# Seven products for the last MLP group too, and two of four operand sums by adding transfers

## The chip, the cores and the metric

The kernel runs on one core of a Trainium2 chip. The metric is the device time of one execution in microseconds; the kernel before has a median of 2015.0 us over three runs (2014.59 to 2015.04). The engines are named as in the profile: PE (TensorE, matrix products; PEld its weight loads), DVE (VectorE), ACT (ScalarE), POOL (GpSimd), SP (SyncE, which issues transfers). A line of the program is written L802.

## The reference

Two layers of an encoder on 256 tokens of width 2048, all in float32. Each layer normalises, projects, runs three kinds of attention, projects back, and then adds a squared-ReLU MLP; a last normalisation follows. The change is in the second product of the MLP, with `w_down`:

```python
for l in range(DEPTH):
    ...
    x = x + jnp.einsum('bse,ed->bsd', mix, w_o[l])
    h = rmsnorm(x, norm_mlp[l])
    u = jax.nn.relu(jnp.einsum('bsd,df->bsf', h, w_up[l]))
    x = x + jnp.einsum('bsf,fd->bsd', u * u, w_down[l])
return rmsnorm(x, norm_final)
```

`w_up[l]` is 2048 x 8192 and `w_down[l]` 8192 x 2048.

## The kernel before

**Numbers.** PE multiplies in a reduced float32 format. To keep float32 accuracy each operand is held as a high part (rounded to that format) and a low part (what is left), and a product is three matmuls: high x high, low x high, high x low. A weight tile of 128 x 1024 is loaded raw (512 KB, tile `wraw`, five buffers), split by ACT, which makes the high part (`whi`, L988), and by DVE, which makes the low part (`wlo = raw - whi`, L989); `whi` and `wlo` have three buffers each.

**Steps.** All weight work is one list of steps, carried out in order by one loop over it. At step i the loads up to step i+6 have been issued, the splits up to i+2, and the preparations (`prep`) up to i+4; then the step's matmuls are issued, and small pieces of other work follow (transposes, attention). The order in which the instructions then stand on each engine is set by a scheduler that moves independent instructions past each other; each engine carries out its own in that order.

**The MLP.** The 8192 hidden columns are cut into eight groups of 1024. `up_steps(g)` makes group g in four pieces q of 256 columns (four steps each, 16 steps in all, L691 and L696); an evacuation on ACT and DVE gives `uT[q]`, the squared activations as high and low part. `down_steps` multiplies a group by `w_down` in the plain way, one 512-column block j of the output at a time (four steps of 12 matmuls, L477), and adds the result to `x` (L739). Groups run one behind the other: while group g goes through `w_down`, group g+1 goes through `w_up`.

**Seven products.** In groups 0 to 6 the output columns 0 to 1023 (j = 0 and 1) are done another way, in `strassen_steps`. The operand is taken as 2 x 2 blocks A11 to A22 (two blocks of tokens, two halves of the rows) and the weight as B11 to B22, and the product is formed from seven block products (P1 to P7, two steps of six matmuls each, L802) in place of eight. For that, sums of blocks are needed on both sides. Those of the activations (`sums_of`, tiles `sT`) are made by DVE and ACT in the evacuation of each piece q, but not for q of 28 and over, which belong to group 7. Those of the weights are four DVE sums of 128 x 1024 for each of two halves h: B12 onto B11 (L815), B22 + B11 (`t2`, L817), B22 onto B12 (L821), and B21 onto `t2` (L832). The blocks are loaded into tiles of their own: B11 into `spare`, the others into `side` (four buffers). Three PSUM banks collect the products (`a` and `d`, the two halves of the tile `S`, and `b`); after each product DVE adds a bank to `x` or subtracts it (L782). The eight plain steps of j = 2 and 3, and the 16 steps of `up_steps(g+1)`, lie between the steps of the seven products, by the list `order` (1 is a step of a product, 0 another one).

**Group 7** goes through `w_down` the plain way for all four column blocks, after everything else. When a column block of `x` is complete, `layer_end` starts what follows: in layer 0 the transposes for the next layer, in layer 1 the squares and the gain of the last normalisation. The very last column block of layer 1 is done one token block at a time, so that the output can begin early.

Of the kernel before, what the change touches and what calls it, by code (L numbers as in the profile page):

```python
# [23 lines left out]
P = 128  # L24
D = 2048
# [18 lines left out]
def tile_trunk(ctx: ExitStack, tc: tile.TileContext, x_in, w_in, w_o, w_up, w_down,  # L44
# [459 lines left out]
    def layer_steps(l):  # L504
# [152 lines left out]
        def up_steps(g):  # L657

            out_, evacs = [], []
            for q in range(4 * g, 4 * g + 4):  # L660
                box = {}

                def evac(q=q, box=box):
# [14 lines left out]
                    if q < 28:  # L678
                        sums_of(q, a)
# [40 lines left out]
        def down_steps(g, js):  # L720
            out_ = []
            for j in js:
                box = {}
                for k in range(4):
                    def mm(wh, wl, j=j, k=k, box=box):
                        if k == 0:
                            box["b"] = [mm_bank(), mm_bank()]
                            box["w"] = []
                        final = l == L - 1 and g == 7 and j == 3
                        hts = [uT[4 * g + k]] * 2  # L730
                        mode_b(box["b"], hts, wh, wl, [0, 1], k == 0, k == 3, blocks=(0,) if final else (0, 1),
                               lo_last=g < 7)
                        box["w"].append((hts, wh, wl))
                        if k < 3:
                            return

                        def evac(t):
                            xs = x[:, t, j * 512:(j + 1) * 512]
                            nc.vector.tensor_add(xs, xs, box["b"][t])  # L739
                        if final:  # L740
                            evac(0)
                            final_block(0)
                            tail = [mm_bank(), mm_bank()]
                            for c in range(2):
                                cols = slice(c * 256, c * 256 + 256)
                                for i, (hts, vh, vl) in enumerate(box["w"]):
                                    mode_b([None, tail[c]], hts, vh[:, :, cols], vl[:, :, cols], [0, 1],
                                           i == 0, i == 3, n=256, blocks=(1,))
                                xs = x[:, 1, 1536 + c * 256:1792 + c * 256]
                                nc.vector.tensor_add(xs, xs, tail[c][:, 0:256])  # L750
                                square_cols(1, 1536 + c * 256, 256, fin["ss"][:, 7 + c:8 + c])
                            final_block(1)
                            return
                        evac(0)
                        evac(1)
                        if g == 7:
                            layer_end(l, j)
                    out_.append(Step(w_down[l, (g * 4 + j) * 4 + k], 2, 512, None, mm, fourth=g == 7))
            return out_

        def strassen_steps(g):
# [5 lines left out]
            raw, t2, box = {}, {}, {}  # L767
# [11 lines left out]
            def evac(bank, t, j, sign):  # L779
# [5 lines left out]
            plan = [("P1", "A11", "a", True, (0, 0, 1)), ("P6", "S2", "a", False, (1, 0, 1)),  # L785
                    ("P7", "S3", "d", True, (1, 1, -1)), ("P5", "S1", "a", False, (1, 1, -1)),
                    ("P3", "S4", "a", False, (0, 1, -1)), ("P2", "A12", "b", True, (0, 0, 1)),
                    ("P4", "A22", "d", False, (1, 0, 1))]
            out_ = []
            for name, lf, bk, fresh, dst in plan:  # L790
                for h in range(2):
                    def mm(wh, wl, name=name, lf=lf, bk=bk, fresh=fresh, dst=dst, h=h):
# [12 lines left out]
                        if h == 1:  # L805
                            evac(o, *dst)
                    loads, prep, get = [], None, None
# [11 lines left out]
                    elif name == "P7":  # L819
                        def prep(h=h):  # L820
                            nc.vector.tensor_add(raw["B12", h], raw["B12", h], raw["B22", h])  # L821
# [353 lines left out]
```

## Time and profile before

| | |
|---|---|
| median of three runs | 2015.0 us (2014.59 to 2015.04) |
| profiled execution | 2015.19 us, of which the span of its instructions is 2013.4 us |
| PE busy | 2000.6 us, 10264 matmuls |
| DVE busy | 1618.2 us |
| ACT busy | 1200.9 us |
| POOL busy | 290.6 us, none of it in the MLP's groups |
| HBM read | 377.34 MB |

The span is what the profile counts from; a few microseconds around it belong to the time as well (2015.19 - 2013.4 = 1.8 us). The MLP of layer 0 runs from about 319 to 1006 us, that of layer 1 from 1317 to 2005 us, and a middle group takes 85.5 us. Matmuls are pipelined, so one's own duration (about 390 ns) is longer than the time from one start to the next, which is what counts.

### The profile page before, as it was taken

What the parts mean: (1) busy time and instruction counts of PE and PEld (TensorE: products, weight loads), DVE (VectorE), ACT (ScalarE), POOL (GpSimd) and SP (SyncE); (2) the same over time, 40 slices, a digit from 0 to 9 for tenths busy, and PEclk for the clock granted to TensorE, in tenths of its full rate; (3) what the DMA queues carried; (4) which work ended last, traced back from release to release, by engine and by line L of the source; (5) the groups of instructions that cost most, each with busy time, mean ns of one, the idle gap of its engine ahead of it and who ended that gap; (6) DMA issues with size and microseconds to landing.
All of it is one profiled execution on the core that took longest, in us unless ns stands there. A gap on an engine that the chain in (4) does not pass through costs nothing.

```text
span 2013.4 us, 27963 instructions
## 1 busy us (share of the span) xinstructions
PE 2000.6 (99%) x10264; PEld 1706.0 (85%) x10264; DVE 1618.2 (80%) x2112; ACT 1200.9 (60%) x1732; POOL 290.6 (14%) x336
## 2 busy tenths in 40 slices
PE   9999999999999999999999999999999999999998
PEld 7888888888888888888888888888888888888887
DVE  6677877879888898887657688778888888888875
ACT  6667756565555556555656677565655556555554
POOL 0684520000000000000008745100000000000001
PEclk9999999999999999999999999999999999999999
DMA  7745655565575656656666456555665756657554
GB/s 276 226 154 162 209 170 190 168 217 193 178 228 170 219 184 192 215 172 198 189 184 200 152 176 198 176 189 179 192 215 170 231 167 210 205 169 233 166 167 156
DMA packets 110102, 384.97 MB, mean 191 GB/s; under 512 B 12515, under 2 KB 16867, under 8 KB 109964
## 3 DMA queue, kind: packets, MB, share of 16 engines
q1 hardware_dynamic: 109532, 382.08, 59.8%
q8 instruction: 81, 1.33, 0.3%
q10 hardware_dynamic: 432, 1.10, 0.2%
q14 instruction: 57, 0.47, 0.1%
HBM read 377.34 MB, written 2.11 MB: 188 GB/s over the span
## 4 chain that ended last, share of the span: by engine, by line
PE 98%; ACT 1%; DVE 0%; issue 0%; DMA 0%; SPq 0%; DVEq 0%; POOLq 0%; POOL 0%
PE mm L477 44%; PE mm L691 23%; PE mm L696 12%; PE S L802 11%; PE mm L802 2%; PE tr L392 1%; PE tr L411 1%; PE S L355 1%; PE S L354 1%; PE tr L221 1%; PE tr L404 0%; ACT big L372 0%; PE tr L267 0%; DMA x<-in_x_dram 0%; PE tr L283 0%
## 5 line engine op out<-in xcount | busy, mean ns | idle before, releaser
L989 DVE TENSOR_TENSOR wlo<-wraw,whi 128x1024 fp32r<-128x1024 f32 (+1 forms) x531 | 654.6, 1236 | 212.5 <-ACT whi L988 209.9
L988 ACT CAST whi<-wraw 128x1024 fp32r<-128x1024 f32 (+1 forms) x531 | 556.7, 1051 | 418.1 <-PE mm L691 170.2
L477 PE MATMUL mm<-whi,big 128*128 128x512 f32 (+1 forms) x2252 | 643.8, 386 | 0.5 <-ACT whi L988 0.5
L691 PE MATMUL mm<-big,whi 128*128 128x512 f32 x2048 | 509.5, 391 | 0.0
L477 PEld LDWEIGHTS mm<-whi,big 128*128 128x128 f32 x2252 | 418.6, 188 | 83.5 <-ACT whi L988 2.5
L691 PEld LDWEIGHTS mm<-big,whi 128*128 128x128 f32 x2048 | 377.1, 188 | 74.1
L477 PE MATMUL mm<-wlo,big 128*128 128x512 f32 (+1 forms) x1126 | 374.9, 384 | 0.0
L696 PEld LDWEIGHTS mm<-big,wlo 128*128 128x128 f32 x2048 | 279.4, 190 | 20.0
L696 PE MATMUL mm<-big,wlo 128*128 128x256 f32 x2048 | 285.5, 282 | 0.0
L477 PEld LDWEIGHTS mm<-wlo,big 128*128 128x128 f32 x1126 | 211.8, 188 | 39.6
L802 PE MATMUL S<-whi,big 128*128 128x512 f32 x672 | 182.2, 393 | 0.0
L477 PE MATMUL mm<-spare,big 128*128 128x512 f32 (+1 forms) x678 | 157.8, 381 | 0.0
L988 ACT CAST whi<-side 128x1024 fp32r<-128x1024 f32 x84 | 88.2, 1050 | 95.2 <-PE mm L691 77.8
L477 PEld LDWEIGHTS mm<-spare,big 128*128 128x128 f32 x678 | 122.3, 188 | 23.2
L802 PEld LDWEIGHTS S<-whi,big 128*128 128x128 f32 x672 | 119.1, 189 | 18.7
L989 DVE TENSOR_TENSOR wlo<-side,whi 128x1024 fp32r<-128x1024 f32 x84 | 102.7, 1223 | 37.5 <-ACT whi L988 37.1
L257 POOL TENSOR_TENSOR sm<-sm,mhalf 128x2 f32<-128x2 f32 (+2 forms) x14 | 15.3, 1092 | 793.7 <-DVE sm L252 773.9
L988 ACT CAST whi<-big 128x1024 fp32r<-128x1024 f32 x56 | 59.0, 1053 | 85.1 <-DVE big L817 36.4
L870 POOL TENSOR_TENSOR x<-x,big 128x512 f32<-128x512 f32 x6 | 8.6, 1451 | 669.5 <-ACT mid L877 669.5
L802 PE MATMUL S<-wlo,big 128*128 128x512 f32 x336 | 103.9, 390 | 0.0
L383 POOL TENSOR_SCALAR big<-big,sm 128x256 f32<-128x256 f32 x128 | 90.3, 723 | 3.0
L989 DVE TENSOR_TENSOR spare<-wraw,spare 128x1024 fp32r<-128x1024 f32 x54 | 70.2, 1299 | 22.2 <-ACT spare L988 21.7
(151 smaller groups left out, 2081.3 us busy)
## 6 DMA issues: line engine op xcount, KB each, us to landing
wraw<-in_w_up_dram SPq DMA_DIRECT2D x256, 512.0 KB, 4.1
wraw<-in_w_down_dram SPq DMA_DIRECT2D x144, 512.0 KB, 3.7
wraw<-in_w_in_dram SPq DMA_DIRECT2D x119, 512.0 KB, 3.8
side<-in_w_down_dram SPq DMA_DIRECT2D x84, 512.0 KB, 4.2
wraw<-in_w_o_dram SPq DMA_DIRECT2D x64, 512.0 KB, 3.6
spare<-in_w_down_dram SPq DMA_DIRECT2D x28, 512.0 KB, 4.2
side<-in_rpb_dram SPq DMA_DIRECT2D x32, 174.8 KB, 5.1
side<-avec SPq DMA_DIRECT2D x8, 384.0 KB, 5.4
```

The lines of the kernel that those rows point to most:

```text
L221: tr = nc.tensor.transpose(psv[:, kk, t, :], x[:, t, c0:c0 + P], ident).ins
L354: nc.tensor.matmul(o, st, u.kh[:, kh, :], start=True, stop=False)
L355: nc.tensor.matmul(o, st, u.kl[:, kh, :], start=False, stop=True)
L383: nc.gpsimd.tensor_scalar(p[:, s, :], p[:, s, :], rs[:, s:s + 1], 1.0, op0=ALU.mult, op1=ALU.mult)
L392: nc.tensor.transpose(ps[:, c * P:(c + 1) * P], u.p[:, s, kb * P:(kb + 1) * P], ident)
L411: nc.tensor.matmul(ps, u.V[:, kb, u.kv, :, :], pt[:, kb, :], start=n == 0, stop=n == 3)
L477: return nc.tensor.matmul(banks[t][:, 0:n], a, (wl if part == "hl" else wh)[:, i, :], start=first and i == 0 and part == "hh", stop=last a ...
L691: nc.tensor.matmul(box["b"][fs], wh[:, kk, fs * P:(fs + 1) * P], ht, start=s == 0 and kk == 0, stop=False, skip_group_check=True)
L696: nc.tensor.matmul(box["b"][fs][:, 0:256], wl[:, kk, fs * P:(fs + 1) * P], ht[:, 0:256], start=False, stop=s == 3 and kk == 3, skip_group_ ...
L802: nc.tensor.matmul(o, ops[i][a], w[:, i, :], skip_group_check=True, start=fresh and h == 0 and i == 0 and a == 0 and w is wh, stop=h == 1 ...
L988: act = nc.scalar.copy(h[:, part], w[:, part]).ins
L989: last_lo[0] = nc.vector.tensor_sub(lo[:, part], w[:, part], f(h[:, part])).ins
```

## The change

Group 7's columns 0 to 1023 are done by seven products as well. For that its rows' sums are made for all q, and its weights are packed like the other groups'. Group 6's plain half (j = 2 and 3) is taken out of group 6, where only the 16 steps of `up_steps(7)` now lie between the products, and is put between the products of group 7: j = 2 of groups 6 and 7 as one accumulation of eight steps, then j = 3 of group 6; j = 3 of group 7 stays last. The column blocks are thereby complete in another order: 2, 1, 0, 3.

In all groups two of the four sums of weights are no longer made by DVE. B12 is added onto B11 in its tile, and B21 onto `t2`, by transfers that add to what they find (`on_top`), issued by POOL. B12 and B21 are also needed by themselves, so each is now transferred twice. The products' order becomes P1, P2, P7, P6, P5, P3, P4.

```diff
-                    if q < 28:
-                        sums_of(q, a)
+                    sums_of(q, a)
...
-        def down_steps(g, js):
-            out_ = []
-            for j in js:
-                box = {}
-                for k in range(4):
-                    def mm(wh, wl, j=j, k=k, box=box):
...
+        def down_steps(gs, j):
+
+            out_, box = [], {}
+            tiles = [(g, k) for g in gs for k in range(4)]
+            final = l == L - 1 and gs == (7,)
+            for n, (g, k) in enumerate(tiles):
+                def mm(wh, wl, g=g, k=k, n=n):
...
-            plan = [("P1", "A11", "a", True, (0, 0, 1)), ("P6", "S2", "a", False, (1, 0, 1)),
-                    ("P7", "S3", "d", True, (1, 1, -1)), ("P5", "S1", "a", False, (1, 1, -1)),
-                    ("P3", "S4", "a", False, (0, 1, -1)), ("P2", "A12", "b", True, (0, 0, 1)),
+            plan = [("P1", "A11", "a", True, (0, 0, 1)), ("P2", "A12", "b", True, (0, 0, 1)),
+                    ("P7", "S3", "d", True, (1, 1, -1)), ("P6", "S2", "a", False, (1, 0, 1)),
+                    ("P5", "S1", "a", False, (1, 1, -1)), ("P3", "S4", "a", False, (0, 1, -1)),
                     ("P4", "A22", "d", False, (1, 0, 1))]
+
+            def on_top(tile, par, j, h):
+
+                nc.gpsimd.dma_start(tile, src(par, j, h).rearrange("p (k n) -> p k n", k=2), accum_op=ALU.add)
...
                         if h == 1:
                             evac(o, *dst)
+
+                            if g == 7 and name in ("P3", "P4"):
+                                layer_end(l, dst[1])
...
+                    elif name == "P2":
+                        def prep(h=h):
+                            assert ("P1", h) in done
+                            on_top(raw["B11", h], 0, 1, h)
+                    elif name == "P7":
+                        loads = [(("B12", h), src(0, 1, h), None), (("B22", h), src(1, 1, h), None)]
+
+                        def prep(h=h):
+                            nc.vector.tensor_add(raw["B12", h], raw["B12", h], raw["B22", h])
+                        get = lambda h=h: raw["B12", h]
                     elif name == "P6":
-                        loads = [(("B12", h), src(0, 1, h), None), (("B22", h), src(1, 1, h), None)]
-
                         def prep(h=h):
-                            nc.vector.tensor_add(raw["B11", h], raw["B11", h], raw["B12", h])
                             t2[h] = big(F32, 2, 512)
                             nc.vector.tensor_add(t2[h], raw["B22", h], raw["B11", h])
                         get = lambda h=h: t2[h]
...
+                    elif name == "P5":
+                        def prep(h=h):
+                            assert ("P6", h) in done
+                            on_top(t2[h], 1, 0, h)
                         get = lambda h=h: raw["B11", h]
...
                     else:
-                        def prep(h=h):
-                            nc.vector.tensor_add(t2[h], raw["B21", h], t2[h])
                         get = lambda h=h: t2[h]
...
-                    stp = Step(None, 2, 512, None, mm, fourth=False, prep=prep, raw=get,
+                    stp = Step(src(1, 0, h) if name == "P2" else None, 2, 512, None, mm, fourth=False, prep=prep,
+                               raw=operand if get else None,
                                loads=[(raw, k, v, w) for k, v, w in loads])
...
         steps.extend(up_steps(0))
-        for g in range(7):
-            ss = down_steps(g, (2, 3)) + up_steps(g + 1)
+        for g in range(8):
+
+            if g < 6:
+                ss = down_steps((g,), 2) + down_steps((g,), 3) + up_steps(g + 1)
+            elif g == 6:
+                ss = up_steps(7)
+            else:
+                ss = down_steps((6, 7), 2) + down_steps((6,), 3) + down_steps((7,), 3)
             hs = strassen_steps(g)
 
             order = [0, 0]
             for p_ in range(7):
-                order += [1, 0, 1] + ([0, 0] + [0] * (p_ in (1, 3, 5)) if p_ < 6 else [])
+                order += [1, 0, 1]
+                if p_ < 6:
+                    order += [0] * (2 if g < 6 else g == 6) + [0] * (g != 6 and p_ in (1, 3, 5))
+            order += [0] * (len(ss) - order.count(0))
...
-        steps.extend(down_steps(7, range(4)))
```

How the instructions move is shown at three places. A row is its line, its operation and its tiles, with the number of each buffer, and what it waits for in brackets (`DMASW` is a transfer that POOL issued, `DMAHW` one that SP issued). The lines of the changed kernel are numbered on: the split on DVE is L1011 (was L989), the sum into `t2` L832 (was L817), the sum B22 onto B12 L827 (was L821), a product's evacuation L783 (was L782), a plain one L740 (was L739), the last part of `sums_of` L716 (was L717).

DVE at the start of group 2 of layer 1 (`spare` holds the two halves of B11, `wlo<-spare` is the split for P1). Before:

```order
1624 L989 TENSOR_TENSOR wlo_14508<-spare_14419,whi_14507 128x1024 [waits DMAHW0_49,Activation_49]
1625 L989 TENSOR_TENSOR wlo_14530<-wraw_14441,whi_14529 128x1024 [waits DMAHW7_49,PE_49,Activation_49]
1626 L676 TENSOR_TENSOR big_14482<-mid_14475,big_14482 128x512 [waits Activation_49]
1627 L712 TENSOR_TENSOR mid_14485<-mid_14475 128x256
1628 L815 TENSOR_TENSOR spare_14419<-spare_14419,side_14525 128x1024 [waits DVE_49]
1629 L713 SCALAR_TENSOR_TENSOR mid_14485<-mid_14485,mid_14475 128x128 [waits DVE_49]
1630 L989 TENSOR_TENSOR wlo_14548<-spare_14453,whi_14547 128x1024 [waits PE_49,Activation_49]
1631 L714 SCALAR_TENSOR_TENSOR mid_14485<-mid_14485,mid_14475 128x128 [waits DVE_49]
1632 L989 TENSOR_TENSOR wlo_14563<-wraw_14492,whi_14562 128x1024 [waits DMAHW0_49,PE_49,Activation_49]
1633 L717 TENSOR_TENSOR big_14489<-mid_14485,big_14489 128x512 [waits Activation_49]
1634 L817 TENSOR_TENSOR big_14567<-side_14527,spare_14419 128x1024
```

And now:

```order
1617 L1011 TENSOR_TENSOR wlo_14555<-spare_14466,whi_14554 128x1024 [waits Activation_49]
1618 L1011 TENSOR_TENSOR wlo_14575<-wraw_14488,whi_14574 128x1024 [waits DMAHW7_49,PE_49,Activation_49]
...
1623 L1011 TENSOR_TENSOR wlo_14593<-spare_14500,whi_14592 128x1024 [waits DMAHW0_49,PE_49,Activation_49]
1624 L716 TENSOR_TENSOR big_14536<-mid_14532,big_14536 128x512 [waits Activation_49]
1625 L1011 TENSOR_TENSOR wlo_14606<-wraw_14539,whi_14605 128x1024 [waits DMAHW0_49,PE_49,Activation_49]
1626 L832 TENSOR_TENSOR big_14802<-side_14678,spare_14466 128x1024 [waits DMASW0_49]
1627 L1011 TENSOR_TENSOR wlo_14625<-wraw_14552,whi_14624 128x1024 [waits DMAHW1_49,PE_49,Activation_49]
1628 L832 TENSOR_TENSOR big_14839<-side_14711,spare_14500 128x1024 [waits DMASW1_49]
1629 L783 TENSOR_TENSOR x<-x,S_14596 128x512 [waits PE_49]
1630 L1011 TENSOR_TENSOR wlo_14638<-wraw_14572,whi_14637 128x1024 [waits DMAHW2_49,Activation_49]
```

The sum L815 is gone; the sums into `t2` (L832) stand in the same place as before, nine and five rows behind the splits of P1, and wait for the transfers that add B12 onto those same tiles. The same holds in groups 1 to 5 of both layers.

DVE at the start of group 7 of layer 1, which had no products before (its rows were plain splits and evacuations). Now:

```order
2027 L1011 TENSOR_TENSOR wlo_18178<-spare_18089,whi_18177 128x1024 [waits DMAHW0_49,PE_49,Activation_49]
...
2035 L713 SCALAR_TENSOR_TENSOR mid_18168<-mid_18168,mid_18158 128x128 [waits DVE_49]
2036 L832 TENSOR_TENSOR big_18311<-side_18229,spare_18089 128x1024 [waits DMASW4_49]
2037 L716 TENSOR_TENSOR big_18172<-mid_18168,big_18172 128x512 [waits Activation_49]
2038 L1011 TENSOR_TENSOR wlo_18217<-spare_18123,whi_18216 128x1024 [waits DMAHW2_49,PE_49]
2039 L1011 TENSOR_TENSOR wlo_18232<-wraw_18136,whi_18231 128x1024 [waits DMAHW0_49,PE_49,Activation_49]
2040 L1011 TENSOR_TENSOR wlo_18251<-wraw_18175,whi_18250 128x1024 [waits DMAHW1_49,PE_49,Activation_49]
2041 L783 TENSOR_TENSOR x<-x,S_18220 128x512 [waits PE_49]
2042 L1011 TENSOR_TENSOR wlo_18266<-wraw_18195,whi_18265 128x1024 [waits DMAHW2_49,Activation_49]
2043 L832 TENSOR_TENSOR big_18341<-side_18263,spare_18123 128x1024 [waits DMASW5_49]
2044 L1011 TENSOR_TENSOR wlo_18278<-wraw_18214,whi_18277 128x1024 [waits DMAHW3_49,PE_49,Activation_49]
```

Here the first sum stands ahead of the split for the second half of P1 (row 2038), and the second transfer can start only behind that split. Group 0 of each layer has the same order up to the second split; there two plain evacuations follow the second sum.

PE in group 7 of layer 1, where P5 (`wlo_18441`) is followed by P3 (`whi_18450`) in the same half of `S`. Now:

```order
8982 L807 MATMUL S_18220<-wlo_18441,big_18017 128x512 [waits DVE_49]
8983 L807 MATMUL S_18220<-wlo_18441,big_18172 128x512
8984 L477 MATMUL mm_18454<-whi_18470,big_17279 128x512 [waits Activation_49]
8985 L477 MATMUL mm_18454<-whi_18470,big_17279 128x512
8986 L477 MATMUL mm_18455<-whi_18470,big_17279 128x512 x2
8987 L807 MATMUL S_18220<-whi_18450,big_17706 128x512 [waits DVE_49]
8988 L807 MATMUL S_18220<-whi_18450,big_17866 128x512
```

Four matmuls of the next plain step have been moved ahead of P3, whose first matmul waits for DVE's evacuation of P5; in the other groups a whole step of `w_up` or a plain one lies between.

82 lines of the change are left out of this document (39 added, 43 removed).

## The prediction

> **What bounds the kernel now.** I read the page first, then the waits of the matrix engine (PE), then the busy times by stretch of the MLP.
>
> ```profile
> span 2013.4 us, 27963 instructions
> PE 2000.6 (99%) x10264; PEld 1706.0 (85%) x10264; DVE 1618.2 (80%) x2112; ACT 1200.9 (60%) x1732; POOL 290.6 (14%) x336
> PE 98%; ACT 1%; DVE 0%; issue 0%; DMA 0%; SPq 0%; DVEq 0%; POOLq 0%; POOL 0%
> ...
> PE tr L267 <- ACT big L533: 2.3, 2, 1.2
> PE mm L999 <- DVE warm L996: 1.6, 1, 1.6
> PE mm L477 <- ACT whi L988: 0.5, 1, 0.5
> PE tr L221 <- DMA x<-in_x_dram: 0.5, 1, 0.5
> ```
>
> The chain that ended last is PE for 98%, and all waits of PE that the profile knows come to 4.9 us. None of them lies in an MLP stage. So time is won by issuing fewer matmuls, and lost as soon as PE has to wait for an operand. Beside it VectorE (DVE) is the engine that could become the bound:
>
> ```profile
> 633.40:718.90 85.50, 85.50 (x437) 73.11 (x436) 73.69 (x91) 49.16 (x59) 0.00 (x0) 1.00 0.61 197
> 889.90:975.00 85.10, 85.10 (x436) 72.80 (x435) 67.39 (x74) 46.36 (x55) 0.00 (x0) 1.00 0.62 192
> 964.10:1006.00 41.90, 41.90 (x199) 34.96 (x198) 27.13 (x34) 24.73 (x41) 0.00 (x0) 1.00 0.62 191
> ```
>
> These are one middle group, the stretch of group 6, and group 7 of layer 0 (columns: length, PE, weight loads, DVE, ScalarE, GpSimd, clock, DMA share, GB/s). PE is busy throughout at full clock; DVE is at 73.69 of 85.50, 86%.
>
> **The matmuls removed.** The price of a step is read off PE's own order of time in that middle group:
>
> ```profile
> 637.73 1.07 PE L802 MATMUL S<-whi,big 128*128 128x512 f32 x4
> 638.63 0.62 PE L802 MATMUL S<-wlo,big 128*128 128x512 f32 x2
> 639.09 1.98 PE L477 MATMUL mm<-whi,big 128*128 128x512 f32 x8
> 640.90 1.07 PE L477 MATMUL mm<-wlo,big 128*128 128x512 f32 x4
> 641.80 1.07 PE L802 MATMUL S<-whi,big 128*128 128x512 f32 x4
> ```
>
> From start to start, a step of a product (six matmuls) takes 639.09-637.73 = 1.36 us, a plain step (twelve) 641.80-639.09 = 2.71 us; one matmul is 2.71/12 = 0.226 us either way. Columns 0 to 1023 of group 7 were 8 plain steps, 96 matmuls; they become 14 product steps, 84 matmuls. That is 12 matmuls a layer, 24 in all: 24 x 0.226 = **5.4 us** off PE. Moving group 6's plain half, and merging it with group 7's for one column block, removes no matmul. The other edits (two of four sums as accumulating transfers) remove DVE work, which nobody waited for; by itself that is worth nothing.
>
> **Does DVE keep up in group 6?** There the plain half is gone, so only up steps lie between the products, and the operand sums for group 7's rows, which nobody made before, are added. DVE's pace, from its order of time:
>
> ```profile
> 638.61 1.22 DVE L989 TENSOR_TENSOR wlo<-wraw,whi 128x1024 fp32r<-128x1024 f32 x1
> 639.74 1.22 DVE L989 TENSOR_TENSOR wlo<-big,whi 128x1024 fp32r<-128x1024 f32 x1
> ...
> 643.33 1.22 DVE L821 TENSOR_TENSOR side<-side,side 128x1024 f32<-128x1024 f32 x1
> 644.47 0.68 DVE L782 TENSOR_TENSOR x<-x,S 128x512 f32<-128x512 f32 x1
> 645.06 1.22 DVE L989 TENSOR_TENSOR wlo<-wraw,whi 128x1024 fp32r<-128x1024 f32 x1
> ```
>
> A 128x1024 split or sum costs 1.14 us from start to start, an evacuation 0.59. The middle group has the sums already, so I start from it: 73.69 minus 8 plain splits (9.1), 4 plain evacuations (2.4) and 4 sums (4.6) leaves 57.6 us of DVE, against PE's 85.5 - 8 x 2.71 = 63.8 us. That is 90%: full, but not the bound. Group 7 has plain steps of 2.71 us between its products and fewer evacuations, so it is lighter. I take no loss here; the bound above is a rival.
>
> **The transfers' latency: the unknown that decides.** A sum `L832` (before: `L817`) now waits for a transfer that GpSimd issues, and that can only start when the split of the first product has read the tile. DVE works in order, so everything behind the sum waits too. The rows of the changed order stand in the part on the change. Call T the time from the end of that split to the landing, and count from the start of the group's first plain step (M); S is a product step.
>
> Group 7 runs M0 0, M1 2.71, S 5.42, M2 6.78, S 9.49, S 10.85, M3 12.21, S 14.92, M4 16.28. The split of the first S needs the buffer that is freed at 0, plus 0.16 of matmul drain (a matmul takes 0.39 and follows after 0.226), and is over by 1.45. The sum then starts at 1.45+T. Behind it stand the sum itself (1.14), one evacuation piece (0.60) and the split of the product's second half (1.22), at whose end, 4.41+T, the second transfer can go. It lands at 4.41+2T; behind it come the second sum and M4's split (1.14+1.22). PE needs that split at 16.28+1.81 = 18.09 (the low parts come 1.81 us into a plain step, 639.09 to 640.90). So PE doesn't wait while 2T is at most 11.32, **T at most 5.7 us**. Group 0 has its second product later but two evacuations in between: 4.41+2T+1.14+1.18+1.22 against 19.44, the same 5.7. Beyond it PE loses 2 us for each us of T, in groups 0 and 7 of both layers: 8 us per us. In groups 1 to 5 the split of the second half is paced by PE (over at 6.8) and the second sum has only four instructions between; 6.8+T+1.14+0.59+1.22 must be at most 16.27+0.90, so T up to 7.4 us is free there, and beyond it ten groups lose 1 us each per us. In group 6 more than 20 instructions lie between, so it is safe.
>
> No transfer of this kind is in the trace. The nearest rows:
>
> ```profile
> side<-in_w_down_dram SPq DMA_DIRECT2D x84, 512.0 KB, 4.2
> ...
> q1 hardware_dynamic: 109532, 382.08, 59.8%
> ```
>
> Below: as a plain load of the same bytes, 4.2 us. Above: everything twice, 8.4 us. In between: the tile must be read as well as the source, so the transfer proper counts twice. A packet took 0.598 x 16 x 2013.4/109532 = 0.176 us, and 512 KB are 128 packets over 16 engines, 8 each, 1.4 us. So T is about 4.2+1.4 = 5.6 us (estimate), which I take because only the moving part doubles: just inside the limit. The queues carry it: four more loads a group are 2.1 MB in 85.5 us, 25 GB/s on 197 at a share of 0.61.
>
> The Trainium skill (DMA: Bandwidth & Descriptors, Anatomy of one DMA) puts a transfer issued by GpSimd at 2.0 us plus its bytes at 436 GB/s, 3.2 us for these, and its Collectives: The Full Stack (The bandwidth ceiling) says an adding transfer reads two sources at half the rate; an estimate from both is 4.4 us, and the sum would stay as it is, with more room. The row of 4.2 us for a transfer that adds nothing says that this is short under this load.
>
> **A bank that is handed on.** In group 7 product P5 is followed at once by P3 in the same bank, where before two steps or more lay between. Four matmuls of the plain step are put between them (0.90 us); P5's evacuation needs 0.16 of drain and 0.68. Between 0 and 0.2 us is lost if DVE is free, up to 1.1 more if it is inside a split. I take 0.2 a layer, **+0.4 us**.
>
> **The sum.** -5.4 + 0.4 = -5.0 us. The profiled execution took 2015.19 us with a span of 2013.4, so the span should come to 2008.4; against the median 2015.0 that is **2010.0 us**.
>
> **The rivals.**
>
> (1) T is a little over the limit, say 6.3: 8 x 0.6 = 4.8 us come back, 2014.8 us, no change. For it: other loads share the queues. Against it: a load is seen to land in 4.2 us beside those same loads.
>
> (2) The transfer is late by the engine that issues it, and the kernel gets slower. GpSimd is seen to be held up:
>
> ```profile
> L383 POOL TENSOR_SCALAR big<-big,sm x128: 468/478/2571, 67.8 to 1260.8; 128x256 f32<-128x256 f32 x128
> ```
>
> The same small operation takes 478 ns in the middle and up to 2571: 2.1 us of delay at worst. T = 5.6+2.1 = 7.7 gives 8 x 2.0 + 10 x 0.3 = 19 us, 2015.0-5.0+19 = 2029 us. It decides from T = 6.9 on (8 x 1.2 = 9.6, more than 5.0 + 4.0). Against it: in the MLP GpSimd has nothing else to do (0.00 in the windows above). The Trainium skill (SBUF — State Buffer, Who interferes with whom) has DVE and GpSimd share a port pair that one of them holds for a whole instruction, so that descriptors can't be written meanwhile; it exempts two-input sums, whose claim on the pair is only for reading. By the lock T would grow by a DVE instruction of 1.22 us to 6.8, about 2018.8 us; by the exemption nothing changes.
>
> (3) DVE becomes the bound in group 6. Its waits for ScalarE come on top:
>
> ```profile
> DVE wlo L989 <- ACT whi L988: 9.4, 12, 1.6
> ACT whi L988 <- PE mm L691: 19.1, 16, 1.7
> ```
>
> If 30/38 of those 9.4 us recur, 57.6+7.4 = 65.0 against 63.8, 1.2 us a layer: 2010.0+2.4 = 2012.4 us, no change. Against it, the second row: ScalarE itself waits for PE to give buffers back, so these waits are mostly slack.
>
> **How the numbers follow.** Forecast 0.50, with a range of its own from 2009.0 to 2011.0; rival 1 0.20; rival 2 0.25; rival 3 0.05. This kernel's runs agree so well that 0.2%, 4.0 us, is what a measurement can tell from no change. Below 2011.0 is faster: the forecast's 0.50. Rivals 1 and 3 are within it: 0.25. Rival 2 is slower: 0.25. The range goes from 2008.9 (all of the 5.4 us and the spread of the runs, with a little over) to 2022, T = 7.2; above that lies about 0.13, below about 0.04.
>
> **What would show it.** Right: 24 fewer matmuls, PE's waits in the MLP below 1 us, the sums `L832` waiting little or, in groups 0 and 7, some us that PE doesn't see, transfers of GpSimd landing in 5 to 6 us. Wrong: rows of PE waiting for DVE `wlo`, with `L832` behind GpSimd's transfers ahead of them: in four places (rival 1) or in all groups but 6 (rival 2). For rival 3 PE waits in group 6 alone, with DVE above 95% there. Wrong altogether would be a matmul that costs more or less than 0.226 us.

## The result and the profile after

The changed kernel takes **2045.69 us** (median of four runs, 2043.21 to 2048.85) against 2014.85 us for the kernel before: ratio 1.0154, 95% interval 1.0142 to 1.0166. It is slower by 1.5%, where a gain of 5 us was forecast; the time lies above the predicted range. The profiled execution took 2043.21 us with a span of 2041.4, 28.0 us more than before. Its page, the lines that answer to those shown of before:

```profile
span 2041.4 us, 28168 instructions
PE 2006.7 (98%) x10240; PEld 1703.1 (83%) x10240; DVE 1592.9 (78%) x2110; ACT 1216.3 (60%) x1752; POOL 352.6 (17%) x400
...
q0 software_dynamic: 9216, 33.56, 10.0%
...
spare<-in_w_down_dram POOLq DMA_DIRECT2D x32, 512.0 KB, 6.6
big<-in_w_down_dram POOLq DMA_DIRECT2D x32, 512.0 KB, 5.9
```

The 24 matmuls are gone (10264 to 10240), DVE has less to do (1618.2 to 1592.9 us), and yet PE stands still. The last two lines give the median time from issue to landing of the adding transfers: 6.6 us onto `spare`, 5.9 onto `t2`. The waits of the changed kernel (us in total, times, longest):

```profile
DVE big L832 <- DMA spare<-in_w_down_dram: 64.7, 28, 4.2
...
PE mm L807 <- DVE wlo L1011: 11.1, 10, 1.6
...
PE mm L477 <- DVE wlo L1011: 9.9, 5, 2.5
```

DVE waits 28 times for a transfer, always at the sum `t2 = B22 + B11` (L832), and PE waits 15 times for a low part that DVE makes (a sixteenth wait, in a matmul onto `S`, is 0.5 us). These are the rows that the prediction named as a sign of its being wrong. The chain can be read in group 1 of layer 0. DVE's order of time (start, duration, instruction, in brackets the idle time before it and what ended it):

```profile
455.96 1.22 DVE L1011 TENSOR_TENSOR wlo<-spare,whi 128x1024 fp32r<-128x1024 f32 x1
...
459.95 1.22 DVE L1011 TENSOR_TENSOR wlo<-spare,whi 128x1024 fp32r<-128x1024 f32 x1
...
463.38 1.23 DVE L832 TENSOR_TENSOR big<-side,spare 128x1024 f32<-128x1024 f32 x1 [0.48 <-DMA spare<-in_w_down_dram]
464.53 1.22 DVE L1011 TENSOR_TENSOR wlo<-wraw,whi 128x1024 fp32r<-128x1024 f32 x1
469.60 1.23 DVE L832 TENSOR_TENSOR big<-side,spare 128x1024 f32<-128x1024 f32 x1 [3.85 <-DMA spare<-in_w_down_dram]
470.74 0.68 DVE L783 TENSOR_TENSOR x<-x,S 128x512 f32<-128x512 f32 x1
471.34 1.22 DVE L1011 TENSOR_TENSOR wlo<-wraw,whi 128x1024 fp32r<-128x1024 f32 x1
```

GpSimd's order of time in the same stretch:

```profile
457.48 0.86 POOL L793 DMA_DIRECT2D spare<-in_w_down_dram  x1 [45.21 <-DVE wlo L1011]
461.46 0.87 POOL L793 DMA_DIRECT2D spare<-in_w_down_dram  x1 [3.12 <-DVE wlo L1011]
```

And PE's, where the gap is:

```profile
470.30 1.07 PE L807 MATMUL mm<-whi,big 128*128 128x512 f32 x4
472.62 0.73 PE L807 MATMUL mm<-wlo,big 128*128 128x512 f32 x2 [1.25 <-DVE wlo L1011]
```

The split of B11's first half ends at 457.18, GpSimd issues 0.3 us later, and the transfer has landed by 463.38: T, from the end of the split to the landing, is 6.2 us. The second split ends at 461.17, the issue follows 0.3 us later, and the landing is at 469.6: T is **8.4 us**. DVE idles 3.85 us before the second sum, the split behind it ends at 472.56, and PE starts its low part at 472.62, 1.25 us late.

**Where the 28.0 us are.** From PE's order of time in the profiled execution, the fastest of the four, I took every pair of matmuls in the MLP whose starts lie over 0.5 us apart, less the normal 0.226:

| part | us |
|---|---|
| 24 matmuls fewer | -5.4 |
| groups 0 and 7 of both layers (2.0, 2.35, 2.3, and 0.7 + 2.6) | +10.0 |
| groups 1 to 5 of both layers, ten gaps of 0.9 to 1.8 | +12.7 |
| end of layer 1, two gaps (0.9 and 1.3) | +2.3 |
| three stretches in which the granted clock was 0.5 | +4.6 |
| the first matmul behind each of the 17 gaps: 0.335 us to the next start in place of 0.226 | +1.8 |
| what is left, spread over the program in no one place | +2.0 |

One of the stretches at half clock, beside one at full clock and the stretch of group 6 (columns: length, PE, weight loads, DVE, ScalarE, GpSimd, clock, DMA share, GB/s):

```profile
387.50:390.90 3.40, 3.40 (x10) 2.63 (x9) 3.14 (x4) 1.04 (x1) 0.00 (x0) 0.50 0.95 349
391.00:400.00 9.00, 9.00 (x45) 7.58 (x44) 5.52 (x6) 3.58 (x4) 0.00 (x0) 1.00 0.69 239
...
886.00:945.00 59.00, 59.00 (x318) 51.04 (x317) 52.87 (x69) 37.93 (x48) 3.49 (x4) 1.00 0.79 233
```

Group 6 itself has no gap: PE is busy for all of its 59 us, DVE for 52.87.

### The profile page after: what moved, and what is told of

It reads as the page before. It is cut to its first block, busy times and chain, and to the rows that moved or that the text cites. A ratio compares the mean times of both kernels' runs of the same rounds, so it can differ in the third digit from the quotient of the medians.

```text
span 2041.4 us, 28168 instructions
## 1 busy us (share of the span) xinstructions
PE 2006.7 (98%) x10240; PEld 1703.1 (83%) x10240; DVE 1592.9 (78%) x2110; ACT 1216.3 (60%) x1752; POOL 352.6 (17%) x400
## 3 DMA queue, kind: packets, MB, share of 16 engines
q0 software_dynamic: 9216, 33.56, 10.0%
## 5 line engine op out<-in xcount | busy, mean ns | idle before, releaser
L1010 ACT CAST whi<-wraw 128x1024 fp32r<-128x1024 f32 (+1 forms) x553 | 579.8, 1051 | 471.6 <-PE mm L477 175.6
L1011 DVE TENSOR_TENSOR wlo<-wraw,whi 128x1024 fp32r<-128x1024 f32 (+1 forms) x553 | 679.1, 1237 | 197.5 <-ACT whi L1010 193.8
L477 PE MATMUL mm<-whi,big 128*128 128x512 f32 (+1 forms) x2172 | 616.2, 387 | 0.5 <-ACT whi L1010 0.5
L807 PE MATMUL S<-whi,big 128*128 128x512 f32 x768 | 210.8, 396 | 0.8 <-DVE x L783 0.8
L793 POOL DMA_DIRECT2D spare<-in_w_down_dram x32 | 28.1, 877 | 762.3 <-DVE wlo L1011 678.9
L793 POOL DMA_DIRECT2D big<-in_w_down_dram x32 | 27.7, 867 | 505.8 <-DVE wlo L1011 497.7
L1010 ACT CAST whi<-side 128x1024 fp32r<-128x1024 f32 x64 | 67.3, 1051 | 68.6 <-PE mm L690 43.4
L1011 DVE TENSOR_TENSOR wlo<-side,whi 128x1024 fp32r<-128x1024 f32 x64 | 78.5, 1227 | 34.0 <-ACT whi L1010 33.9
L1011 DVE TENSOR_TENSOR wlo<-big,whi 128x1024 fp32r<-128x1024 f32 x64 | 79.2, 1238 | 28.5 <-ACT whi L1010 28.4
L1010 ACT CAST whi<-spare 128x1024 fp32r<-128x1024 f32 x64 | 67.4, 1054 | 53.8 <-PE mm L690 42.4
```

Of the source, the lines that this page charges most:

```text
L477: return nc.tensor.matmul(banks[t][:, 0:n], a, (wl if part == "hl" else wh)[:, i, :], start=first and i == 0 and part == "hh", stop=last a ...
L793: nc.gpsimd.dma_start(tile, src(par, j, h).rearrange("p (k n) -> p k n", k=2), accum_op=ALU.add)
L807: nc.tensor.matmul(o, ops[i][a], w[:, i, :], skip_group_check=True, start=fresh and h == 0 and i == 0 and a == 0 and w is wh, stop=h == 1 ...
L1010: act = nc.scalar.copy(h[:, part], w[:, part]).ins
L1011: last_lo[0] = nc.vector.tensor_sub(lo[:, part], w[:, part], f(h[:, part])).ins
```

## The experiments

The theory at the start: DVE, which works in order, waits at L832 for a transfer that is later than 5.6 us, and PE for what stands behind the sum. The rivals: the added traffic as such; the issue by GpSimd; the new order of groups 6 and 7. The kernel before took 2014.88 us beside the first four runs, 2015.16 beside e5 to e7, 2014.98 beside e8 to e11 and 2015.06 beside e12.

**e4, a transfer that copies.** It leaves the two sums out; all else stays.

```diff
-                nc.gpsimd.dma_start(tile, src(...), accum_op=ALU.add)
+                nc.gpsimd.dma_start(tile, src(...))
```

> The changed kernel with the 64 transfers of GpSimd copying and not adding (so B12 replaces B11 + B12, and B21 replaces t2: the sums of weights are wrong, all else stays). If adding is what makes them late (a packet took 0.328 us, a plain load's 0.18), eight packets per engine save 1.2 us and the first lands about 4.9 us after its split, the second, less in the way of other loads, 6 to 7; PE's gaps shrink to a few tenths and the time comes to 2010 to 2018 us. If the issue by GpSimd makes them late (1.6 us to the first packet), they land as late as now and the time stays above 2035 us.

Measured: **2012.87 us** (ratio 0.9990, 0.9981 to 0.9999). Not adding takes 32.8 us off the changed kernel, with every issue, byte and wait in place. The page of e4:

```profile
q0 software_dynamic: 9216, 33.56, 5.4%
...
spare<-in_w_down_dram POOLq DMA_DIRECT2D x32, 512.0 KB, 3.8
big<-in_w_down_dram POOLq DMA_DIRECT2D x32, 512.0 KB, 3.9
```

And of its waits, the row of the sum:

```profile
DVE big L832 <- DMA spare<-in_w_down_dram: 2.8, 7, 0.5
```

The copies land 3.8 us after their issue, sooner than SP's loads of the same size (4.2 onto `side` in this run), so the issue by GpSimd is not what makes the adding ones late. A packet's mean time is 0.100 x 16 x 2041.4/9216 = 0.354 us where it adds and 0.054 x 16 x 2010.8/9216 = 0.189 where it copies. Onto `spare`, the first transfer of a pair took 5.5 to 6.2 us from issue to landing when adding, the second 7.1 to 8.5; copying, both took 3.8 at the median. Why the second is later shows in three stretches of the changed kernel: the first transfer almost alone on the engines, its end beside SP's loads, and the second one beside SP's loads:

```profile
459.00:462.00 3.00, 3.00 (x15) 2.49 (x14) 2.93 (x7) 2.33 (x3) 0.54 (x1) 1.00 1.03 160
462.00:463.40 1.40, 1.40 (x8) 1.17 (x7) 0.92 (x2) 0.61 (x1) 0.33 (x1) 1.00 1.00 345
...
466.00:469.50 3.50, 3.50 (x17) 2.92 (x16) 0.00 (x0) 1.05 (x1) 0.00 (x0) 1.00 0.97 322
```

The DMA engines are full in all three (shares 1.03, 1.00, 0.97). With almost only adding packets they move 160 GB/s, with mostly loads 345: adding goes at half the rate and fills the engines meanwhile, and the second transfer takes its turns with SP's loads. By the packet records of this group the first transfer's packets are on the engines for 3.8 us while loads move 0.2 MB, the second's for 5.4 us while loads move 0.8 MB. DVE is idle throughout the last stretch.

**e3, the transfers without the new group 7.** The kernel before, with the changed kernel's `strassen_steps` in groups 0 to 6; of its text only

```diff
-                            nc.vector.tensor_add(raw["B11", h], raw["B11", h], raw["B12", h])
+                            on_top(raw["B11", h], 0, 1, h)
...
-                            nc.vector.tensor_add(t2[h], raw["B21", h], t2[h])
+                            on_top(t2[h], 1, 0, h)
```

with the new order of products and places of loads that belong to it.

> The kernel before with the adding transfers and the new order of products in groups 0 to 6; group 7 plain as before. If the wait for the transfers costs the time, the gaps that the changed kernel shows in groups 0 to 5 come back: 4.3 us in the two groups 0, 12.9 in groups 1 to 5, some 0.25 us of restart behind each of 12, and none, one or two stretches of half clock at 1.6 us: 2035 us (2032 to 2039). If the loss sits in groups 6 and 7, 2015 us.

Measured: 2030.87 us (ratio 1.0081, 1.0068 to 1.0095), just below the range. The gaps are back in the groups that have the transfers, with group 7 plain and group 6 in its old place, so the new order isn't the cause. They were smaller in the profiled execution, the fastest of the four (2028.2 us): ten of them, 11.1 us together, and no half clock; the transfers landed after 6.0 us at the median onto `spare`, not 6.6. The kernel's runs lay between 2028.2 and 2035.6; only the fastest has a trace, so what the others lost on top is not shown.

**e1, the sum before the transfer.** The sum is formed from what is there already, and the transfer comes after it:

```diff
-                        def prep(h=h):
-                            assert ("P1", h) in done
-                            on_top(raw["B11", h], 0, 1, h)
...
-                            nc.vector.tensor_add(t2[h], raw["B22", h], raw["B11", h])
+                            nc.vector.tensor_add(t2[h], raw["B12", h], raw["B11", h])
+                            assert ("P1", h) in done
+                            on_top(raw["B11", h], 0, 1, h)
```

(B12's tile holds B12 + B22 by then.)

> The changed kernel with one difference: t2 is formed by DVE as (B12 + B22) + B11, ahead of the transfer, and only then the transfer adds B12 onto B11. All 64 adding transfers, their bytes and the issuing engine stay; no DVE instruction waits for one of them any more. If the loss is DVE's in-order wait for the transfer (L832 in the changed kernel: 64.7 us over 28 waits), the 15 gaps of PE in the MLP go, and the span comes to 2008 to 2009.5, the time to 2010 us (2009 to 2012). If the added traffic itself (33.5 MB more, on queues that carry 58%) or the new order of groups 6 and 7 costs the time, it stays near 2040 us.

Measured: 2026.03 us (ratio 1.0056, 1.0043 to 1.0068). 19.7 us are gained with all the traffic in place, and no gap is left in groups 0 to 5. The transfers onto `spare` were not quicker here (8.5 us at the median, by the page of e1, against 6.6): what is gone is that DVE waits for them. So the in-order wait is shown as the cause of those gaps. But 2010 was expected. Two rows of the waits of e1:

```profile
DVE side L825 <- DMA side<-in_w_down_dram: 10.3, 7, 5.5
...
PE S L807 <- DVE x L783: 9.1, 3, 5.3
```

In group 6 PE now stands still for 5.4 and 3.0 us, and DVE waits up to 5.5 us for a load onto `side`.

**e5, the sum and the transfer earlier still.** As e1, but in the preparation of P7, right behind B12 + B22, so that the tiles of B12 come free as early as in the change.

> As e1 (t2 = (B12 + B22) + B11 by DVE, then B12 added onto B11 by the transfer), but the sum and the transfer stand in the preparation of P7, right behind the sum B12 + B22, so that each tile of B12 comes free as early as in the changed kernel and the transfers of a group do not come in one bunch. By the waits: no DVE instruction stands closer than 11 us of DVE work behind a transfer, so the gaps of PE go, those of e1 in group 6 (5.4 and 3.0 us) too, and what is left is what e4 shows: 2012.5 us (2011.5 to 2014.5). If the adding transfers cost time just by filling the DMA engines (other loads standing still meanwhile), PE waits for late loads in several groups and it stays above 2018 us.

Measured: 2024.16 us (ratio 1.0045, 1.0032 to 1.0057), a miss again: the group 6 gaps stay (4.2 and 3.2 us). GpSimd's order of time in e5 there:

```profile
901.84 0.87 POOL L793 DMA_DIRECT2D spare<-in_w_down_dram  x1 [66.02 <-DVE big L827]
903.58 0.87 POOL L793 DMA_DIRECT2D spare<-in_w_down_dram  x1 [0.86 <-DVE big L827]
906.75 0.87 POOL L793 DMA_DIRECT2D big<-in_w_down_dram  x1 [2.30 <-DVE wlo L1010]
```

Two stretches of e5, in the columns shown before:

```profile
904.00:909.00 5.00, 5.00 (x28) 4.26 (x27) 4.19 (x5) 2.84 (x5) 1.32 (x2) 1.00 0.91 192
909.00:914.00 5.00, 4.25 (x23) 3.33 (x21) 0.00 (x0) 2.10 (x2) 0.00 (x0) 1.00 1.05 272
```

And DVE's wait for the loads onto `side`, in all:

```profile
DVE side L825 <- DMA side<-in_w_down_dram: 13.8, 9, 6.0
```

Three adding transfers are issued within 5 us where the changed kernel spreads its four of this group over 31 (892.84 to 923.46). The DMA engines are full, and a load onto `side` issued at 904.26 lands at 914.05, 9.8 us later; DVE does nothing from 909 to 914. Here the rival of the traffic is right, in one group; with the transfers of this group spread as in the change, e9 below has no gap there.

**e6, a plain step between P5 and P3** of group 7, on top of e5.

```diff
-                    order += [0] * (2 if g < 6 else g == 6) + [0] * (g != 6 and p_ in (1, 3, 5))
+                    order += [0] * (2 if g < 6 else g == 6) + [0] * (g != 6 and p_ in ((1, 3, 5) if g < 6 else (1, 3, 4)))
```

> e5 with one plain step of group 7 moved from behind P3 to between P5 and P3, so that bank a is not handed on at once. If the hand-over is what e4 shows at the end of layer 1 (0.95 us at 1975.65, PE waiting for the evacuation L783, which waits behind a split of 2.15 us), this is 0.9 to 1.3 us faster than e5. If that gap only moves, the same as e5 within 0.4 us.

Measured: 2023.91 us (ratio 1.0042, 1.0029 to 1.0054), the same as e5. In place of gaps of 0.9 and 1.3 us at the end of layer 1 there are 1.1 and 0.6 elsewhere in that end: moving the step alone gains nothing that can be measured.

**e7, the sum later.** The other way out of the wait: the change's sum directly ahead of P6's split.

```diff
-                        def prep(h=h):
+                        def get(h=h):
                             t2[h] = big(F32, 2, 512)
                             nc.vector.tensor_add(t2[h], raw["B22", h], raw["B11", h])
-                        get = lambda h=h: t2[h]
+                            return t2[h]
```

> The changed kernel with one difference: the sum t2 = B22 + (B11 + B12) is made by DVE directly ahead of P6's split and not two steps earlier; the transfers, their place and their bytes are the changed kernel's. In groups 0 to 6 the second sum then stands over 30 DVE rows behind the second split of P1; in group 7 it keeps its 5 rows (the order of instructions says so). If the in-order wait decides, the gaps of groups 0 to 5 (17.2 us) go and the two of group 7 (2.4 and 2.6 us, and up to two stretches of half clock) stay: 2018 us (2016 to 2021). If the traffic decides, it stays near 2040 us.

Measured: **2067.63 us** (ratio 1.0265, 1.0251 to 1.0279), where 2018 was expected. Its waits:

```profile
PE S L807 <- ACT whi L1010: 32.4, 14, 2.6
DVE big L832 <- DMA spare<-in_w_down_dram: 17.1, 15, 4.5
```

The waits for the transfers fell from 64.7 to 17.1 us, as expected, and the gaps that they caused in groups 0 to 5 are gone. But sum, cast and split now follow one another behind whatever DVE has ahead of the sum, and PE waits for the cast 14 times, 2.3 us each. The two steps of lead were needed. The run says nothing against the theory, and it is no test of its size.

**e2, all sums by DVE.** The changed kernel with `strassen_steps` of the kernel before, and in it only

```diff
                             evac(o, *dst)
+                            if g == 7 and name in ("P3", "P4"):
+                                layer_end(l, dst[1])
```

> Seven products in all eight groups as in the change, with group 6's plain half moved, but all four sums of weights by DVE and the order of products as in the kernel before; no adding transfer. If the transfers alone cost the time and DVE keeps up, 2010 us (2009 to 2012): the matmuls saved. If DVE is the bound in group 6 (57.6 us and two more sums a half, 4.6, are 62.2 of 63.8 us there, and 7.4 us of waits for ScalarE on top), PE loses up to 5.8 us a layer there, 2015 to 2022 us.

Measured: 2022.68 us (ratio 1.0039, 1.0025 to 1.0053), just above the range given for DVE as the bound. Two stretches of e2, in group 6 and at the start of group 7:

```profile
892.00:906.00 14.00, 12.75 (x67) 10.37 (x66) 13.86 (x19) 8.55 (x12) 0.00 (x0) 1.00 0.37 116
946.00:957.00 11.00, 8.62 (x38) 6.87 (x37) 11.00 (x15) 5.36 (x8) 0.00 (x0) 1.00 0.15 52
```

DVE is busy for 13.86 of 14.0 us and all of 11.0, and PE loses 1.25 and 2.4 us. So the sums have to leave DVE in this part of the program, if the plain half is to leave group 6.

**e8 and e9, adding transfers only where DVE is full.** Groups 0 to 5 as in the kernel before, group 6 as in the change, and group 7 with DVE sums (e8) or as in e5 (e9). The line of e9 (in e8 its last name is `by_dve`):

```diff
-            hs = strassen_steps(g)
+            hs = (by_dve if g < 6 else by_transfer if g == 6 else sum_first)(g)
```

> Adding transfers where DVE is short, and nowhere else: groups 0 to 5 exactly as in the kernel before (DVE sums, its order of products), group 6 as in the changed kernel (in whose profile PE has no gap in group 6), group 7 by seven products with DVE sums. If the adding transfers cost the time by DVE's in-order wait in groups 0 to 5 and 7 and are worth their price only in group 6, where e2 shows DVE busy without a break, the gaps of e2 before group 7 go too; what stays is the end of layer 1: 2012 us (2011 to 2013.5), below both kernels. If group 7 needs the transfers as well (e2: 0.8 us at 972), 2013 to 2015 us.

> As e8, but group 7 as in e5 (t2 formed first, then B12 added onto B11 by a transfer). By the gaps in the profiles (none in group 6 of the changed kernel, none in group 7 of layer 0 in e5) 2012 to 2013 us. If group 6's transfers push back the loads of group 7, as in e5 (4.2 and 3.2 us), 2018 us or more.

Measured: e8 **2020.74 us** (ratio 1.0027, 1.0017 to 1.0036), e9 **2013.05 us** (ratio 0.9990, 0.9981 to 0.9999). e8 is a miss: group 6 is clean, but the gap of 2.5 us at the start of group 7 stays, with DVE busy for all of the 11.5 us around it. With 16 adding transfers in place of 64, e9 has no gap before the end of layer 1. It is faster than both kernels, than the kernel before by 1.9 us.

**e10 and e11, the end of layer 1.** e10 is e4's kernel again; e11 is e4 without GpSimd's multiplications by the last gain.

> e4 again on this chip, for the rows of its end: gaps of PE at the end of layer 1 of about 1 and 1.3 us, 2013 us.

> e4 (transfers that copy and do not add) without GpSimd's multiplications by the last gain (L892), which is left out of the output for column blocks 0 to 2. If the two gaps that e4 keeps at the end of layer 1 (1.18 and 1.57 us from start to start) come from GpSimd slowing DVE's splits (2.1 to 2.3 us in place of 1.22 beside L892), they go and the time falls by 2.3 to 3 us against e4, to 2010 us. If the hand-over of bank a alone makes the first one, only the second goes: 2011.4 us.

Measured: e10 2013.07 us (a single run), e11 **2010.67 us** (ratio 0.9978, 0.9968 to 0.9987). The first of the two gaps in e4's orders of time. GpSimd's:

```profile
1970.90 4.20 POOL L892 TENSOR_TENSOR x<-x,big 128x512 f32<-128x512 f32 x2 [6.82 <-ACT mid L899]
```

DVE's, with the split behind which the evacuation waits:

```profile
1974.04 2.15 DVE L1011 TENSOR_TENSOR wlo<-wraw,whi 128x1024 fp32r<-128x1024 f32 x1
1976.11 0.67 DVE L783 TENSOR_TENSOR x<-x,S 128x512 f32<-128x512 f32 x1
```

PE's, at P3:

```profile
1976.84 1.20 PE L807 MATMUL S<-whi,big 128*128 128x512 f32 x4 [0.80 <-DVE x L783]
```

Beside GpSimd's multiplication a split takes 2.15 us in place of 1.22, the evacuation of bank a waits behind it, and P3 for that. Without the multiplications both gaps are gone, and between 1960 and 2000 us no split takes longer than 1.23 us.

The kernel before had the same neighbours, without a loss. What stands ahead of the prediction, that none of GpSimd's time lies in the MLP's groups, doesn't hold for group 7 of layer 1 (columns as before):

```profile
1962.30:2005.50 43.20, 43.20 (x214) 36.60 (x212) 25.48 (x29) 20.34 (x32) 9.14 (x7) 1.00 0.47 150
```

There too a split beside GpSimd was long, 1.95 us, but PE didn't wait for it:

```profile
1985.35 2.87 POOL L870 TENSOR_TENSOR x<-x,big 128x512 f32<-128x512 f32 x2 [8.02 <-ACT mid L877]
...
1987.35 1.95 DVE L989 TENSOR_TENSOR wlo<-wraw,whi 128x1024 fp32r<-128x1024 f32 x1 [1.54 <-ACT whi L988]
```

**e12, the gains by DVE.** e9, with the multiplications made by DVE one column block later:

```diff
-            nc.gpsimd.tensor_mul(xs, xs, gain)
+            owed.append((xs, gain))
...
+    def pay():
+        while owed:
+            xs, gain = owed.pop(0)
+            nc.vector.tensor_mul(xs, xs, gain)
```

(`gain` stands for the slice of the gain's tile; `pay` is called at the start of `final_chunk` and in the third step of the last column block.)

> e9 with the multiplications by the last gain made by DVE one column block later, and not by GpSimd at once (the whole result is computed). If GpSimd beside DVE makes the two gaps at the end of layer 1 (e11: 2.2 us without it), six DVE instructions of 0.6 us fit into group 7 and the time falls from 2013.0 to 2011 us (2010.3 to 2012). If DVE has no room there, other gaps take their place and it stays at 2013 us.

Measured: **2010.41 us** (2010.0 to 2011.07; ratio 0.9977, 0.9968 to 0.9986), the lowest median of all; e11, within 0.3 us of it, leaves the multiplications out. Its page:

```profile
span 2008.7 us, 28062 instructions
PE 1996.3 (99%) x10240; PEld 1702.1 (85%) x10240; DVE 1644.9 (82%) x2164; ACT 1217.4 (61%) x1752; POOL 296.1 (15%) x346
```

Its span is 4.7 us below the kernel before's, and no pair of matmuls in the MLP lies over 0.5 us apart.

## Why the prediction was wrong

**The step that failed is the latency T.** The prediction took 5.6 us, one value for every transfer, as a load's 4.2 plus 1.4 for packets that count twice. A packet does take 1.9 times as long, and a copy's 3.8 us from the issue with 0.3 before it are near the 4.2. But the estimate left out that slow packets fill the DMA engines, that loads wait behind them, and that the second transfer of a pair meets those loads. Its check of the queues, 25 GB/s on 197 at a share of 0.61, was an average over a whole group; in the 10 us of a pair (459.0 to 469.5) the share was 0.94 to 1.03. In the first group T was 6.1 and 7.7, and in groups 1 to 5 the first was 6.0 to 6.5 and the second 7.9 to 8.8. So the sum, which had nothing for this wait, was short of 22.7 us of gaps.

**The mechanism was right, and its limits nearly so.** For groups 0 and 7 the prediction let both transfers together take 11.3 us. With the four pairs measured (13.7, 13.6, 13.75 and 14.6) its own working gives 10.4 us of gaps; 10.0 were found. For groups 1 to 5 it let the second take 7.4 us. With a mean of 8.3 that makes 8.7 us; 12.7 were found, which a limit of 7.0 gives. Pair by pair the traces bear this out: in these ten groups, and in groups 1 to 6 of both layers in e3, PE's gap was the second T less 7.0 us to within 0.02 us (T 7.9, gap 0.9; T 8.8, gap 1.8), and none where T was 7.0 or less. So PE does lose 1 us for each us of T, as the prediction said, from 7.0 and not from 7.4. 19 of the 22.7 us follow from the prediction's working with the measured T in it, the other 4 from those 0.4 us in ten groups.

**Rival 2 in part.** Its sign and its place came true, and its price of 2029 us at T = 7.7 fell 17 us short; its cause did not come true. GpSimd was hardly held up: it issued 0.3 us after the split for 57 of the 64 transfers, 0.5 for six and 1.0 for one, and a copy was as quick as SP's loads. Rival 1, a T a little over the limit, was too small. The Trainium skill (DMA: Bandwidth & Descriptors, Anatomy of one DMA, and Collectives: The Full Stack, The bandwidth ceiling) gave 4.4 us as an estimate; the half rate agrees with 160 against 345 GB/s, but 5.3 us was the shortest landing of the 64.

**What the sum had no term for.** Behind a gap PE lost more than the gap: 4.6 us at half clock and 1.8 in the first matmuls. With the 2.0 us that I can't place, this took the loss from 25 to 33 us. The prediction's loss per us of T had only the gaps.

**DVE relief "worth nothing": wrong as said.** Group 6 did keep up with the transfers, as forecast, at 52.87 of 59 us. But there the transfers pay for it: e2, with the sums on DVE, loses 2022.68 - 2013.05 = 9.6 us against e9. The sums were free to DVE in groups 0 to 5 alone.

**The bank that is handed on.** 0.2 us a layer was taken, with up to 1.1 more if DVE is inside a split. In layer 1 it was 0.9 us, by just that case, and a second gap of 1.3 us came with it; in layer 0 there was none. That GpSimd's multiplications make the splits long was not seen, though the kernel before shows it (1.95 us): the prediction's "in the MLP GpSimd has nothing else to do" rests on windows of layer 0, and in group 7 of layer 1 GpSimd is busy for 9.14 us. The Trainium skill (SBUF — State Buffer, Who interferes with whom) says that a DVE instruction with two inputs in SBUF contends with a GpSimd instruction that reads SBUF; 2.15 against 1.22 us agrees, and the prediction had drawn on that section for the issue of transfers only.

**The matmuls.** 24 x 0.226 = 5.4 us was right: with the other losses taken away, e11 and e12 come out 4.3 and 4.65 us below the kernel before, and 0.4 us above the forecast's 2010.0 in the case of e12.

**When a gap is followed by half clock.** In the changed kernel it came behind three of the five places where matmuls started over 2.0 us apart. The clock records of the kept traces show what sets these three apart. Within a run the half-clock stretches begin a whole number of steps of 3.4133 us from each other: 172 and 296 steps in the changed kernel; 52, 64, 132, 26, 52 and 52 in e7. Laid over the whole run, these steps cut some gaps in two. Twelve gaps of e7 are alike, 2.3 us each. Six of them have over 2.0 us in one step, and half clock follows; six are cut into pieces of at most 1.8 us, and it doesn't. In the six traces with such stretches (the changed kernel, e1, e2, e5, e6, e7) more than 2.1 us of a gap in one step were always followed by half clock (ten gaps), and less than 1.8 never. How the steps lie against the kernel's start differs from trace to trace, so in these runs this part of the loss was luck.

**What stays open.** With 1.9 to 2.1 us in one step it went both ways (six gaps with half clock, two without); these runs don't tell why.

## What to carry to other kernels

Price an asynchronous operand by its latency in its own place, beside the loads that run there, and for each of a chain of transfers; then ask which instruction of an in-order engine waits for it and what stands behind that. If the same value can be formed from data already there, do that first, and let the transfer follow. Use such a transfer only in the stage whose engine is full: in e9, 16 of the 64 gave all of the relief that was needed.

## What the runs showed of the hardware

- A transfer that adds onto its target ran at half rate: 0.354 us a packet against 0.189 for a copy, 160 GB/s with the DMA engines full against 345 with loads. From issue to landing it took 5.3 to 8.5 us in the changed kernel (median 6.1); the copy in e4 3.7 to 5.5 (median 3.9).
- While adding transfers fill the engines, other loads come late: 9.8 us for one of 512 KB in e5, against a median of 4.2 in that run.
- After some gaps of 2.0 to 2.6 us the granted clock was 0.5 for 3.413 us. The Trainium skill (TensorE: Matmul & The Clock Gate, What's actually happening) states a window of that length; that gaps shorter than it suffice is what these runs add.
- Half-clock stretches began on steps of 3.4133 us; a gap was followed by one when about 2 us of it fell into a single step (always above 2.1, never below 1.8).
- Behind a gap the first matmul took 0.335 us to the next start in place of 0.226, at full clock.
- A DVE split took 2.15 us beside a GpSimd multiplication, in place of 1.22.
